# A diffusion layer on one core: modulation steps bound to the matmul units, fewer beside the up-projection and more beside the channel projections

## The chip, the cores and the metric

One Trainium2 chip, one of its cores. The metric is the device time of one execution in microseconds (us); less is better. TensorE (PE) does the matmuls, VectorE (DVE) and ScalarE (ACT) the arithmetic around them, GpSimd (POOL) some of it, SyncE (SP) issues the transfers.

## The reference

One layer over 1024 tokens of width 1024, with 256 context tokens beside them: a half-step SwiGLU feed-forward (ffn1, inner width 2816), a mix of a Fourier group and a two-directional state-space scan (SSD), and a second half-step SwiGLU (ffn2). Each of the three is wrapped in RMS norms and in a modulation that comes from the conditioning vector:

```
mod = (silu(c) @ ada_w + ada_b)           # 9 vectors of 1024
h   = rms_norm(x, g_pre) * (1 + scale) + shift
y   = (silu(h @ w_gate) * (h @ w_up)) @ w_down
x   = x + 0.5 * gate * rms_norm(y, g_post)
```

Everything is computed to float32 accuracy.

## The kernel before

**Products.** A float32 product is made of three matmuls on rounded halves (`mm3`, L461). So every operand is split first: `split` casts the high half on ACT (L198) and subtracts it on DVE for the low half (L199). The up-projection works in 22 *units* of 84 matmuls of 128x512 by a Strassen-like scheme (the products in PSUM `pa` to `pd`); weights come in by `uload`, their sums are made in `usums` (L534 to L537), their splits in `usplit`. `u_first` (L569) is the first DVE addition that takes a unit's products out of PSUM, `u_mid` and `u_late` the rest.

**Start** (L339 to L422). Four iterations i load and transpose token blocks, scale them (L357 on ACT, L359 on DVE), form sums of blocks on DVE (`h_sums`, L396 to L399) and split them (`h_split`): two casts on ACT, 1536 and 2048 wide (L416), and two subtractions (L422), the first on GpSimd, the second on DVE. Then the first products follow (`product(0, p, (i,))`).

**Modulation.** The vectors 0 and 1 are made in the start. The other seven are cut into 14 *u* of 512 columns, made by the generator `ada()`, on DVE. Each u has 8 steps k: a step loads a 128x512 piece of `adaR` (256 KB) into `ring` and multiplies and adds it into an accumulator (L766 for k = 0, else L768), for both streams v if u < 6 and for one after that. When a u is complete, `cut` splits the accumulator (ACT L713, DVE L714), and `end` sums it over the partitions with two matmuls into `pmod` (L720, L721) and writes the vector's place: for mods 2, 5 and 8 with two DMAs (L725, L730), else by DVE into the columns `AB`. Each call of `next(st)` goes one step on. In `ffn_up`, `step()` is called five times per unit; this covers u 0 to 11, until nothing is left. In `ffn_down` one `next(st8)` follows each inner block, for u 12 and 13.

**Down-projection.** `ffn_down` runs three passes over the tokens, tiles (0, 1), (2, 3, 4) and (5, 6, 7), each over the 22 inner blocks f. `down_prep` loads a weight block (512 KB) and a piece of g and splits both, as far ahead as `wring` and `gring` have areas, but never past the end of the pass. After a tile's last block, `post_norm` (L790, L791) reads its PSUM and `pre_scale`, `pre_turn` (L813 transposes, L820) prepare the tile for the mix.

**Channel projections.** `project` runs 24 groups of 24 matmuls (`pch`, 128x256): four token ranges j times six weights i. Each group is copied out by ACT (L986, L988).

**Order.** The program is written in one sequence. A tile scheduler that simulates it fixes each engine's own order of instructions at build time; `high_priority` and `issue_after` bend that order. Every engine then runs its list in order and waits at semaphores.

Of the kernel before, what the change touches and what calls it, by code (L numbers as in the profile page):

```python
# [127 lines left out]
class Kernel:  # L128
# [272 lines left out]
    def h_split(self, i, hb, highs, lows, first):  # L401
# [8 lines left out]
        for o, e in ((0, 3), (3, 7)):  # L410
# [199 lines left out]
    def ffn_up(self, begun, tail, step=lambda: None):  # L610

        n = len(self.ulist)
        for u in range(n):
# [28 lines left out]
            step()  # L642
# [27 lines left out]
    def ffn_down(self, post, step=lambda p, f: None, before=lambda p: None):  # L670

        m = self.m
        P = {}
# [23 lines left out]
    def ada(self, us, ring, acc, sp, scr, ahead, tag="AUX"):  # L697
# [19 lines left out]
        def end(u, v, s):  # L717
            mod, half = 2 + u // 2, u % 2
            P = self.psum("pmod", tag)
# [34 lines left out]
        for n in range(ahead):  # L754
            load(n)
        for n, (u, k) in enumerate(todo):
# [72 lines left out]
    def ffn1(self):  # L829
# [10 lines left out]
        st = self.ada(range(12), ring, acc, sp, scr, 2)  # L840
        st8 = None
# [15 lines left out]
        self.ffn_up(True, tail, lambda: next(st, None))  # L857
# [3 lines left out]
        m.free(self.cc, *self.hfree, *self.wq["S4"])  # L861
# [8 lines left out]
        ring, acc, sp = Ring(m, 512, 2, F32, X2), Ring(m, 512, 1, F32, F0), Ring(m, 1024, 1, FR, X1)  # L870
        st8 = self.ada((12, 13), ring, acc, sp, scr, 1)
        self.pending = []

        def before(p):
            if p == 0:
                state["G"] = self.gload(0)
            if p < 2:
                return

            for _ in st8:  # L880
                pass
            sp.release()
            for r in (self.wring, self.gring):
                for q in r.areas:
                    for s in q:
                        if s[0] is X1:
                            m.free(s)
                r.areas = [q for q in r.areas if q[0][0] is not X1]
            self.gring.areas += [(m.alloc(384, FR, X1), m.alloc(384, FR, Q))]
            state["w"] = [tuple(m.alloc(1024, FR, R0 if i < 2 else X1) for _ in range(2)) for i in range(6)]  # L890
# [3 lines left out]
        def step(p, f):  # L894
            next(st8, None)
# [17 lines left out]

        self.ffn_down(post, step, before)
        for r in (ring, acc, b2, self.graw, self.wraw):
            r.release()
        m.free(state["G"], scr)
# [917 lines left out]
```

## Time and profile before

| | |
|---|---|
| Time, median of 3 runs | 2336.15 us (2334.01 to 2337.88) |
| The profiled execution, its own time | 2346.82 us |
| Its span in the trace | 2344.8 us |
| Mean granted TensorE clock | 0.966 |
| PE / DVE / ACT / POOL busy, share of the span | 92% / 64% / 39% / 18% |

How to read it: busy is the time in which an engine executes. Matmuls are pipelined, so a busy PE can still run below its pace; the count of matmuls per us in a stretch shows that. The granted clock is a share of 2.4 GHz; at 0.5 the engine runs at 1.2 GHz. The rest of the execution's time, 2346.82 - 2344.8 = 2.0 us, lies around the span.

### The profile page before, as it was taken

The numbers are of one execution on the slowest core, as the hardware profiler recorded it, in microseconds if no ns is written. First come the engines' busy times: TensorE is split into PE (matmuls) and PEld (weight loads), VectorE is DVE, ScalarE is ACT, GpSimd is POOL, SyncE is SP. The second block draws the span as 40 slices with busy tenths as digits, with TensorE's granted clock in tenths as the row PEclk, the third lists the DMA queues.
The fourth block names the chain that finished last, engine by engine and source line by source line (L and its number), as shares of the span: only waits on it lengthen the run. The fifth ranks groups of instructions, "written<-read, shape, count | busy, mean of one in ns | idle before, by whom it ended". The sixth has DMA issues, their size and how long they took to land. (4 is left out here: it accounts for less than half of the span.)

```text
span 2344.8 us, 28370 instructions
## 1 busy us (share of the span) xinstructions
PE 2168.8 (92%) x10532; PEld 1805.8 (77%) x10532; DVE 1505.1 (64%) x2226; ACT 924.3 (39%) x1403; POOL 422.6 (18%) x444
## 2 busy tenths in 40 slices
PE   5799999999999899998899987888799999999998
PEld 3577778887778799887888877666688888878886
DVE  6999886656645513348887866787556565656453
ACT  4322223234535433326556545356222222245341
POOL 1100000000212000007776631673000000001010
PEclk9799999999999999999999989999899999999999
DMA  6344553228755501312455445453412222258572
GB/s 259 112 136 153 169 175 99 96 84 276 251 181 192 174 28 47 105 46 90 139 165 178 145 135 166 136 182 122 153 57 85 77 87 75 88 185 275 180 228 88
DMA packets 124827, 329.39 MB, mean 140 GB/s; under 512 B 12928, under 2 KB 43776, under 8 KB 123664
## 3 DMA queue, kind: packets, MB, share of 16 engines
q1 hardware_dynamic: 124688, 327.57, 42.8%
q8 instruction: 83, 1.36, 0.2%
q14 instruction: 56, 0.46, 0.1%
HBM read 273.77 MB, written 53.76 MB: 140 GB/s over the span
## 5 line engine op out<-in xcount | busy, mean ns | idle before, releaser
L198 ACT CAST R<-F 128x1024 fp32r<-128x1024 f32 (+1 forms) x172 | 164.3, 961 | 242.5 <-PE pd L461 75.1
L199 DVE TENSOR_TENSOR R<-F,R 128x1024 fp32r<-128x1024 f32 (+1 forms) x155 | 196.3, 1271 | 79.4 <-ACT R L198 72.7
L207 POOL TENSOR_SCALAR F<-F 128x1 f32<-128x1 f32 x18 | 4.2, 235 | 1279.7 <-ACT F L228 1279.7
L198 ACT CAST Q1a<-F 128x1024 fp32r<-128x1024 f32 (+1 forms) x115 | 129.3, 1130 | 225.8 <-PE pd L461 102.7
L461 PE MATMUL pch<-R 128*128 128x512 f32 (+1 forms) x912 | 172.2, 349 | 13.8 <-DVE X3b L790 4.7
L461 PEld LDWEIGHTS pch<-R 128*128 128x128 f32 x912 | 148.1, 198 | 33.9 <-issue 10.3
L461 PE MATMUL gu<-R 128*128 128x256 f32 (+1 forms) x1152 | 162.2, 299 | 2.7 <-ACT R L198 1.2
L461 PEld LDWEIGHTS gu<-R 128*128 128x128 f32 x1152 | 149.8, 194 | 11.2 <-ACT R L198 1.6
L199 DVE TENSOR_TENSOR Q1a<-F,Q1a 128x1024 fp32r<-128x1024 f32 x93 | 113.5, 1220 | 39.0 <-ACT Q1a L198 38.8
L1253 POOL TENSOR_TENSOR R<-F 128x384 fp32r<-128x384 f32 x128 | 128.6, 1033 | 24.2 <-PE pD L1287 17.5
L461 PE MATMUL y<-Q1a 128*128 128x512 f32 x438 | 107.7, 395 | 0.0
L461 PE MATMUL pa<-R,Q1a 128*128 128x512 f32 x330 | 95.6, 401 | 10.9 <-ACT Q1a L198 9.6
L461 PE MATMUL pa<-R 128*128 128x512 f32 x306 | 87.5, 403 | 14.1 <-ACT R L198 13.3
L461 PE MATMUL y<-Q1a,X3a 128*128 128x512 f32 x360 | 93.2, 404 | 5.5 <-DVE X3b L790 2.6
L768 DVE SCALAR_TENSOR_TENSOR X3b<-X3b,F 128x512 f32<-128x512 f32 x126 | 95.1, 770 | 4.2 <-DMA X3b<-adaR 3.9
L461 PEld LDWEIGHTS y<-Q1a 128*128 128x128 f32 x438 | 83.3, 191 | 18.2
L198 ACT CAST X7a<-F 128x1024 fp32r<-128x1024 f32 (+1 forms) x47 | 57.8, 1231 | 90.9 <-PE pd L461 78.5
L461 PE MATMUL pc<-R,Q1a 128*128 128x512 f32 x286 | 87.6, 401 | 0.7 <-DVE F L604 0.7
L461 PEld LDWEIGHTS y<-Q1a,X3a 128*128 128x128 f32 x360 | 68.9, 193 | 22.9 <-issue 3.0
L461 PE MATMUL pd<-R,Q1a 128*128 128x512 f32 x286 | 84.9, 393 | 0.0
L461 PEld LDWEIGHTS pa<-R,Q1a 128*128 128x128 f32 x330 | 62.1, 191 | 29.1 <-ACT Q1a L198 12.1
L199 DVE TENSOR_TENSOR X7a<-F,X7a 128x1024 fp32r<-128x1024 f32 (+1 forms) x47 | 68.1, 1451 | 24.7 <-ACT X7a L198 24.6
(424 smaller groups left out, 4911.1 us busy)
## 6 DMA issues: line engine op xcount, KB each, us to landing
F<-ffn_wd SPq DMA_DIRECT2D x154, 512.0 KB, 4.3
F<-ffn_w SPq DMA_DIRECT2D x42, 1024.0 KB, 5.4
X3b<-adaR SPq DMA_DIRECT2D x112, 256.0 KB, 2.9
F<-ffn_w SPq DMA_DIRECT2D x44, 512.0 KB, 4.4
F<-w_ch SPq DMA_DIRECT2D x26, 512.0 KB, 4.1
g_d<-X3b SPq DMA_DIRECT2D x22, 512.0 KB, 2.7
g_d<-F SPq DMA_DIRECT2D x20, 512.0 KB
X3b<-g_d SPq DMA_DIRECT2D x44, 192.0 KB, 5.8
```

What stands on the lines that cost most here:

```text
L198: nc.scalar.copy(out=m.r(hi, off, off + n), in_=m.f(src, soff, soff + n))
L199: (E or nc.vector).tensor_tensor(out=m.r(lo, off, off + n), in0=m.f(src, soff, soff + n), in1=m.f(hi, off, off + n), op=ALU.subtract)
L207: V.tensor_scalar(out=mv, in0=ss, scalar1=scale * RSQ_M, scalar2=EPS * RSQ_M, op0=ALU.mult, op1=ALU.add)
L461: self.nc.tensor.matmul(out=outs[c], lhsT=l, rhs=r[c], start=first and ps == 0, stop=last and ps == 2, skip_group_check=again)
L768: V.scalar_tensor_tensor(out=ac, in0=m.f(x), scalar=s, in1=ac, op0=ALU.mult, op1=ALU.add)
L1253: G.tensor_tensor(out=m.r(R, 384 * i, 384 * i + 384).rearrange("p (h l) -> p h l", h=3), in0=self.cst(tri).unsqueeze(1).broadcast_to([128, ...
```

## The change

1. `h_split` makes all low halves on DVE (five instructions come from GpSimd: four iterations, of which the third has two).
2. Beside `ffn_up` only u 0 to 7 are made. Each step is issued under `issue_after(self.mark)`, the mark being the unit's `u_first` addition, and one of the five calls per unit goes.
3. u 8 to 13 are made in `project`, three steps after each group of `pch`; their `pmod` takes PSUM from AUX, then from TR. The loads use three buffers, two ahead.
4. `down_prep` may run on into the next pass. `before(p)` is asked when the preparation reaches pass p.
5. The areas of `wring` and `gring` are kept in a list that rotates, and new ones are put at its front. ffn2's down-projection uses the same code.

```diff
@@ h_split
-                    (nc.gpsimd if o == 0 else nc.vector).tensor_tensor(
+                    nc.vector.tensor_tensor(
@@ u_first
-        self.nc.vector.tensor_tensor(out=U, in0=self.P[u, "B"], in1=U, op=ALU.add)
+        self.mark = self.nc.vector.tensor_tensor(out=U, in0=self.P[u, "B"], in1=U, op=ALU.add).ins
@@ ffn_up
             self.u_mid(u)
-            step()
@@ ffn_down
-            before(p)
...
-                while self.nq < min((p + 1) * NF, p * NF + fs[0] + min(len(self.wring.areas), len(self.gring.areas))):
+                while self.nq < min(len(self.passes) * NF, p * NF + fs[0] + min(len(self.wring.areas), len(self.gring.areas))):
+                    if self.nq % NF == 0 and self.nq not in asked:
+                        asked.add(self.nq)
+                        before(self.nq // NF)
+                        continue
                     self.down_prep()
@@ ada
-            P = self.psum("pmod", tag)
+            P = self.psum("pmod", self.adatag)
...
         for n in range(ahead):
             load(n)
+        yield
@@ ffn1
-        st = self.ada(range(12), ring, acc, sp, scr, 2)
+        self.adatag = "AUX"
+        st = self.ada(range(8), ring, acc, sp, scr, 2)
+        next(st)
+
+        def beside():
+            with self.tc.issue_after(self.mark):
+                next(st, None)
...
-        self.ffn_up(True, tail, lambda: next(st, None))
+        self.ffn_up(True, tail, beside)
...
-        ring, acc, sp = Ring(m, 512, 2, F32, X2), Ring(m, 512, 1, F32, F0), Ring(m, 1024, 1, FR, X1)
-        st8 = self.ada((12, 13), ring, acc, sp, scr, 1)
...
         def before(p):
-            if p == 0:
-                state["G"] = self.gload(0)
...
-            for _ in st8:
-                pass
-            sp.release()
...
+            if p == 2:
+                for r in (self.wring, self.gring):
+                    state.setdefault("x1", []).extend(x for q in r.areas if q[0][0] is X1 for x in q)
+                    r.areas = [q for q in r.areas if q[0][0] is not X1]
         def step(p, f):
-            next(st8, None)
+            if p == 2 and f == 0:
+                m.free(*state["x1"])
+                self.gring.areas.insert(0, (m.alloc(384, FR, X1, True), m.alloc(384, FR, Q)))
+                state["w"] = [tuple(m.alloc(1024, FR, R0 if i < 2 else X1) for _ in range(2)) for i in range(6)]
...
+        state["G"] = self.gload(0)
         self.ffn_down(post, step, before)
@@ pairs
-        self.wring.areas += [tuple(m.alloc(1024, FR, bank) for _ in range(2)) for _ in range(nw)]
+        self.wring.areas[:0] = [tuple(m.alloc(1024, FR, bank) for _ in range(2)) for _ in range(nw)]
@@ project
+        scr, ring, acc, sp = m.alloc(1024, F32, self.F0), Ring(m, 512, 2, F32, self.X2), Ring(m, 512, 1, F32, self.F0), Ring(m, 1024, 1, FR, self.Q)
+        ring.areas.append(m.alloc(512, F32, self.F0))
+        st = self.ada(range(8, 14), ring, acc, sp, scr, 2)
+        next(st)
...
                 if j < 2 and i in (1, 4) and self.pending:
                     self.pending.pop(0)()
+                for _ in range(3):
+                    next(st, None)
...
         self.banks(main=1, PZ=4, TR=2)
+        self.adatag = "TR"
+        for _ in st:
+            pass
@@ class Pairs
-        self.areas, self.i = [], 0
-    next = Ring.next
+        self.areas = []
+    def next(self):
+        self.areas.append(self.areas.pop(0))
+        return self.areas[-1]
```

Three places show how the order moves. First, DVE in the start's fourth iteration, from the split of the third iteration's last part to that of the fourth (`X3b` are modulation pieces and accumulators, `X3a` the fourth iteration's halves). Before:

```order
L766 TENSOR_SCALAR X3b<-X3b,F_61 128x512 x2
L359 TENSOR_SCALAR F_61<-ptr,F_61 128x512
L768 SCALAR_TENSOR_TENSOR X3b<-X3b,F_61 128x512 x2
L396 TENSOR_TENSOR F_61<-F_61 128x512
L768 SCALAR_TENSOR_TENSOR X3b<-X3b,F_61 128x512 x2
L397 TENSOR_TENSOR F_61<-F_61 128x512
L768 SCALAR_TENSOR_TENSOR X3b<-X3b,F_61 128x512 x2
L398 SCALAR_TENSOR_TENSOR F_61<-F_61 128x512
L768 SCALAR_TENSOR_TENSOR X3b<-X3b,F_61 128x512 x2
L399 TENSOR_TENSOR F_61<-F_61 128x512
L768 SCALAR_TENSOR_TENSOR X3b<-X3b,F_61 128x512 x4
L422 TENSOR_TENSOR X3a<-F_61,X3a 128x2048
```

Now:

```order
L422 TENSOR_TENSOR Q1a<-F_61,R_60 128x2048
L359 TENSOR_SCALAR F_61<-ptr,F_61 128x512
L396 TENSOR_TENSOR F_61<-F_61 128x512
L397 TENSOR_TENSOR F_61<-F_61 128x512
L422 TENSOR_TENSOR X3a<-F_61,X3a 128x1536
L398 SCALAR_TENSOR_TENSOR F_61<-F_61 128x512
L399 TENSOR_TENSOR F_61<-F_61 128x512
L422 TENSOR_TENSOR X3a<-F_61,X3a 128x2048
L569 TENSOR_TENSOR F_61<-pb,F_61 128x512
```

The modulation's accumulations, two to four between each of the sums, are gone from here, and the first split (1536 wide) has come in from GpSimd between L397 and L398.

Second, DVE where pass 1 of ffn1's down-projection ends and pass 2 begins (128x1024 to L199 is a weight block, 128x384 a piece of g; L790 and L791 read the finished tiles; L793 and L794 now). Before:

```order
L199 TENSOR_TENSOR X3a<-F_61,X3a 128x1024
L199 TENSOR_TENSOR Q1a<-F_61,Q1a 128x1024 x2
L790 SCALAR_TENSOR_TENSOR X3b<-y,F_61 128x1024
L199 TENSOR_TENSOR R_60<-F_61,R_60 128x1024
L791 TENSOR_TENSOR X3b<-X3b,F_61 128x1024
L199 TENSOR_TENSOR Q1a<-X3b,Q1a 128x384
L199 TENSOR_TENSOR Q1a<-F_61,Q1a 128x1024
L199 TENSOR_TENSOR Q1a<-X3b,Q1a 128x384
L790 SCALAR_TENSOR_TENSOR X3b<-y,F_61 128x1024
L199 TENSOR_TENSOR Q1a<-X3b,X3a 128x384
L791 TENSOR_TENSOR X3b<-X3b,F_61 128x1024
L790 SCALAR_TENSOR_TENSOR X3b<-y,F_61 128x1024
```

Now:

```order
L199 TENSOR_TENSOR Q1a<-X3b,Q1a 128x384
L199 TENSOR_TENSOR Q1a<-F_61,Q1a 128x1024 x2
L199 TENSOR_TENSOR Q1a<-X3b,X3a 128x384
L199 TENSOR_TENSOR Q1a<-F_61,Q1a 128x1024
L793 SCALAR_TENSOR_TENSOR X3b<-y,F_61,X3b 128x1024
L794 TENSOR_TENSOR X3b<-X3b,F_61 128x1024
L199 TENSOR_TENSOR R_60<-F_61,R_60 128x1024
L199 TENSOR_TENSOR Q1a<-X3b,Q1a 128x384
L793 SCALAR_TENSOR_TENSOR X3b<-y,F_61,X3b 128x1024
L794 TENSOR_TENSOR X3b<-X3b,F_61 128x1024
L793 SCALAR_TENSOR_TENSOR X3b<-y,F_61,X3b 128x1024
L794 TENSOR_TENSOR X3b<-X3b,F_61 128x1024
```

Four splits for the next pass now stand ahead of the first tile's addition and three tiles' additions stand closer together; before, the splits for pass 2 stood between and behind these.

Third, PE in the channel projections (`pch`; `ptr` are the transposes of the last tiles; `pmod` the sums of a u). Before:

```order
L461 MATMUL pch<-R_60 128x256 x48
L813 MATMUL ptr<-F_61 128x128 x8
L461 MATMUL pch<-R_60,X3a 128x256 x48
L813 MATMUL ptr<-F_61 128x128 x2
L461 MATMUL pch<-R_60,X3a 128x256 x24
L813 MATMUL ptr<-F_61 128x128 x2
L461 MATMUL pch<-R_60,X3a 128x256 x2
L813 MATMUL ptr<-F_61 128x128 x4
L461 MATMUL pch<-R_60,X3a 128x256 x22
```

Now:

```order
L461 MATMUL pch<-R_60 128x256 x48
L816 MATMUL ptr<-F_61 128x128 x8
L461 MATMUL pch<-R_60,X3a 128x256 x53
L722 MATMUL pmod<-Q1a,R_60 128x512
L461 MATMUL pch<-R_60,X3a 128x256
L723 MATMUL pmod<-Q1a,R_60 128x512
L461 MATMUL pch<-R_60,X3a 128x256 x33
L816 MATMUL ptr<-F_61 128x128 x4
L461 MATMUL pch<-R_60,X3a 128x256 x9
L461 MATMUL pch<-R_60 128x256 x6
L816 MATMUL ptr<-F_61 128x128 x4
L461 MATMUL pch<-R_60 128x256 x39
```

The first two matmuls of `pmod`, for u 8, stand after the 101st and 102nd `pch` matmul; those for the other five u follow at some 85 `pch` matmuls from one to the next (after 189, 274, 360, 439 and 516 of the 576). PE executes its list in order, so `pch` behind a `pmod` waits with it.

## Rows read from the trace of the kernel before

**Rows 1.** The page: span, and busy time of each engine.

```profile
span 2344.8 us, 28370 instructions
PE 2168.8 (92%) x10532; PEld 1805.8 (77%) x10532; DVE 1505.1 (64%) x2226; ACT 924.3 (39%) x1403; POOL 422.6 (18%) x444
```

**Rows 2.** Busy time by stretch: from:to, length, busy us (instructions), clock, DMA, GB/s.

```profile
core 0: us, PE busy (x) PEld busy (x) DVE busy (x) ACT busy (x) POOL busy (x), PEclk, DMA share, GB/s
0.00:92.00 92.00, 48.64 (x272) 31.86 (x273) 70.90 (x115) 35.83 (x41) 14.76 (x9) 0.82 0.54 196
92.00:330.00 238.00, 225.90 (x951) 180.50 (x950) 222.43 (x324) 68.61 (x83) 0.00 (x0) 0.98 0.48 159
330.00:535.00 205.00, 205.00 (x894) 167.67 (x893) 129.65 (x162) 61.70 (x73) 0.00 (x0) 1.00 0.30 99
535.00:618.00 83.00, 79.67 (x336) 63.82 (x335) 55.76 (x74) 38.08 (x56) 10.56 (x28) 0.98 0.88 298
690.00:712.00 22.00, 16.84 (x61) 12.67 (x60) 11.51 (x12) 10.16 (x17) 13.25 (x32) 0.84 0.62 217
799.00:830.00 31.00, 23.28 (x162) 23.07 (x163) 16.09 (x41) 16.52 (x29) 5.40 (x9) 0.83 0.45 141
830.00:885.00 55.00, 55.00 (x457) 54.99 (x457) 8.35 (x14) 14.62 (x32) 0.00 (x0) 1.00 0.10 30
```

**Rows 3.** Timeline of POOL in the start: start us, us, instruction, idle before and releaser.

```profile
32.53 3.50 POOL L422 TENSOR_TENSOR R<-F,R 128x1536 fp32r<-128x1536 f32 x1 [32.09 <-ACT R L416]
75.54 3.58 POOL L422 TENSOR_TENSOR X3a<-F,X3a 128x1536 fp32r<-128x1536 f32 x1 [11.79 <-ACT X3a L416]
```

**Rows 4.** Timeline of DVE in the start.

```profile
30.98 1.75 DVE L199 TENSOR_TENSOR R<-F,Q1a 128x1536 fp32r<-128x1536 f32 x1
32.98 3.60 DVE L396 TENSOR_TENSOR F<-F 128x512 f32<-128x512 f32 x1
36.62 0.69 DVE L397 TENSOR_TENSOR F<-F 128x512 f32<-128x512 f32 x1
...
66.97 2.28 DVE L422 TENSOR_TENSOR Q1a<-F,R 128x2048 fp32r<-128x2048 f32 x1
...
75.75 4.58 DVE L768 SCALAR_TENSOR_TENSOR X3b<-X3b,F 128x512 f32<-128x512 f32 x2
...
87.35 2.28 DVE L422 TENSOR_TENSOR X3a<-F,X3a 128x2048 fp32r<-128x2048 f32 x1
```

**Rows 5.** Timeline of ACT in the start's fourth iteration.

```profile
69.35 1.45 ACT L357 ACTIVATE F<-ptr,F 128x512 f32<-128x512 f32 x2 [3.13 <-DVE Q1a L422]
73.99 1.47 ACT L416 CAST X3a<-F 128x1536 fp32r<-128x1536 f32 x1 [3.19 <-issue]
84.81 1.90 ACT L416 CAST X3a<-F 128x2048 fp32r<-128x2048 f32 x1 [9.35 <-DVE F L399]
```

**Rows 6.** Timeline of PE at the end of the start.

```profile
86.76 0.80 PE L461 MATMUL pb<-X3a,Q1a 128*128 128x512 f32 x1 [6.37 <-ACT X3a L416]
```

**Rows 7.** DVE time of the accumulations (L768) in a stretch of the up-projection.

```profile
110.00:150.00 40.00, 13.69 (x20) 1.00 0.45 152
```

**Rows 8.** Waits of PE, 95 to 535 us: engine, line, releaser, total, times, longest.

```profile
PE pa L461 <- ACT Q1a L198: 9.6, 6, 2.8
```

**Rows 9.** Waits of PE, 535 to 600 us.

```profile
PE pmod L720 <- ACT X3a L713: 3.3, 2, 2.6
```

**Rows 10.** Timeline of DVE in pass 0: first and last of one u's eight accumulations.

```profile
547.15 0.49 DVE L766 TENSOR_SCALAR F<-X3b,F 128x512 f32<-128x512 f32 x1 [2.03 <-DMA X3b<-adaR]
...
566.38 0.75 DVE L768 SCALAR_TENSOR_TENSOR F<-X3b,F 128x512 f32<-128x512 f32 x1
```

**Rows 11.** Waits of PE, 798 to 890 us.

```profile
PE pch L461 <- DVE X3b L790: 4.7, 1, 4.7
PE pch L461 <- ACT F L988: 3.6, 1, 3.6
```

**Rows 12.** The page's DMA issues: transfers, KB each, us from issue to landing.

```profile
X3b<-adaR SPq DMA_DIRECT2D x112, 256.0 KB, 2.9
```

More of the change, by code (lines that the diff above doesn't have):

```diff
@@ L672, in ffn_down @@
         m = self.m
-        P = {}
+        P, asked = {}, set()
         def mm(q, p, i, t):
@@ L694, in ffn_down, with ada @@
                     step(p, f)
-    def ada(self, us, ring, acc, sp, scr, ahead, tag="AUX"):
+    def ada(self, us, ring, acc, sp, scr, ahead):
         m, nc, a = self.m, self.nc, self.a
@@ L855, in tail @@
             self.down_prep()
-        self.ffn_up(True, tail, lambda: next(st, None))
+        self.ffn_up(True, tail, beside)
         for r in (self.ut, self.sg):
             r.release()
-        m.free(self.cc, *self.hfree, *self.wq["S4"])
+        m.free(self.cc, scr, *self.hfree, *self.wq["S4"])
         self.hh = [m.alloc(4096, FR, R0) for _ in range(2)]
@@ L869, in ffn1 @@
         b2 = Ring(m, 1024, 2, F32, X2)
-        ring, acc, sp = Ring(m, 512, 2, F32, X2), Ring(m, 512, 1, F32, F0), Ring(m, 1024, 1, FR, X1)
-        st8 = self.ada((12, 13), ring, acc, sp, scr, 1)
         self.pending = []
         def before(p):
-            if p == 0:
-                state["G"] = self.gload(0)
-            if p < 2:
-                return
-            for _ in st8:
-                pass
-            sp.release()
[L883 to L890, printed above, removed]
+            if p == 2:
+                for r in (self.wring, self.gring):
+                    state.setdefault("x1", []).extend(x for q in r.areas if q[0][0] is X1 for x in q)
+                    r.areas = [q for q in r.areas if q[0][0] is not X1]
         self.wch = []
         def step(p, f):
-            next(st8, None)
+            if p == 2 and f == 0:
+                m.free(*state["x1"])
+                self.gring.areas.insert(0, (m.alloc(384, FR, X1, True), m.alloc(384, FR, Q)))
+                state["w"] = [tuple(m.alloc(1024, FR, R0 if i < 2 else X1) for _ in range(2)) for i in range(6)]
             i = len(self.wch)
@@ L912, in post @@
             self.pending.append(lambda: self.pre_turn(2, m.r(self.hh[c]), m.r(self.hl[c]), 512, (t % 4) * 128, xx, self.full, "AUX", True, V if t > 5 else None))
+        state["G"] = self.gload(0)
         self.ffn_down(post, step, before)
-        for r in (ring, acc, b2, self.graw, self.wraw):
+        for r in (b2, self.graw, self.wraw):
             r.release()
-        m.free(state["G"], scr)
+        m.free(state["G"])
         for r in (self.wring, self.gring):
@@ L924, in pairs @@
         m = self.m
-        self.wring.areas += [tuple(m.alloc(1024, FR, bank) for _ in range(2)) for _ in range(nw)]
-        self.gring.areas += [tuple(m.alloc(384, FR, bank) for _ in range(2)) for _ in range(ng)]
+        self.wring.areas[:0] = [tuple(m.alloc(1024, FR, bank) for _ in range(2)) for _ in range(nw)]
+        self.gring.areas[:0] = [tuple(m.alloc(384, FR, bank) for _ in range(2)) for _ in range(ng)]
     def tok_proj(self, P, n, t, ws):
@@ L1001, in project @@
         self.banks(main=1, PZ=4, TR=2)
+        self.adatag = "TR"
+        for _ in st:
+            pass
+        for r in (ring, acc, sp):
+            r.release()
+        m.free(scr)
         for w in self.wch:
```

1 line of the change is left out of this document (removed).

## The prediction

> **What bounds the kernel now.** I read the page first, then the time by stretch, and last the waits and timelines of the stretches in which something is lost. TensorE is busy in 92% of the span, VectorE in 64% [rows 1], so the end is set by TensorE nearly everywhere, and the change can win only where TensorE runs below its pace. The pace is seen from 330 to 535 us, where the up-projection goes on after the modulation's steps have run out: 894 matmuls in 205 us, 4.36 per us, without a gap and at the full clock [rows 2]. A unit of 84 matmuls then takes 84 / 4.36 = 19.3 us. Held against that pace, the other stretches lose:
>
> - 0 to 92 us: PE is busy 48.6 us, DVE 70.9; the stretch is bound by loads and by the chain over DVE and ACT.
> - 92 to 330 us: 951 matmuls are worth 951 / 4.36 = 218 us; 238 went by, so 20 are lost. VectorE is busy in 222 of the 238 us, with the accumulations among it: 20 in 40 us [rows 7].
> - 535 to 618 us: 336 are worth 77 us, 83 went by: 6 lost, at a DMA share of 0.88.
> - 690 to 712 us: 61 are worth 14 us: 8 lost, and the clock falls to 0.84.
> - 799 to 830 us: 7.7 us of 31 without a matmul, and a clock of 0.83; the same kind of work runs at 457 matmuls in 55 us from 830 on, so 162 are worth 19.5 us: 11.5 lost [all rows 2].
>
> From 885 us on the change touches little: only the down-projection of ffn2 runs through the edited code.
>
> The profiled execution took 2346.8 us, 10.7 more than the median of the three runs, 2336.15. The terms come from the profiled one; I take the sum off both.
>
> **The start: -13 us (bounds -5 and -18).** In the fourth iteration the last split of the third ends at 66.97 + 2.28 = 69.25 us and the fourth's own last split at 87.35 + 2.28 = 89.63 [rows 4]: 20.4 us. Two things fill it. The accumulations stand between the sums in VectorE's list, and one pair of them took 4.58 us [rows 4], where ten accumulations take 6.8 [rows 7], because GpSimd was subtracting from 75.54 to 79.12 [rows 3]. Both go. What is left is a chain: two activations 1.45 and a cast 1.47 [rows 5], to 72.2; the split of 1536 columns, now on VectorE, 1.75 (the same width and form in L199) [rows 4], to 73.9; two sums of 0.69, to 75.3; the cast of 2048, 1.90 [rows 5], to 77.2; the split of 2.28, to 79.5. With half a us for handing over that is 80, 9.6 less than 89.6. TensorE waited for just this cast and split [rows 6], so all of it counts. In the first three iterations one sum each took some 3.6 us in place of 0.69, beside a GpSimd subtraction of 3.5 [rows 3, 4]: 2.9 saved three times, and a split of 1.75 added to VectorE three times, which makes about -3.4. Together -13. The weakest end is the fourth iteration's half, -5, if loads come next in line; the strongest is -18, if the later products no longer meet the low clock of 0.82.
>
> Here a rule speaks against the change. The Trainium skill ("Perfetto Trace Analysis", section "Optimizing Scalar/DVE Operations") says that when VectorE is saturated, moving some work off to ScalarE or even GpSimd may make sense, and adds that GpSimd shares a port with it; the trace agrees with the second half (3.60 against 0.69 us [rows 4]) and I go by that.
>
> **Beside the up-projection: -12 us (bounds -4 and -20).** Removed are the accumulations of u 8 to 11, 32 x 0.68 = 22 us of VectorE, and their cuts; the other 64 are spread: two per step for both streams, at most four steps and so 8 accumulations per unit. Without accumulations VectorE needs, from 92 to 330 us, 222.4 - 238 / 40 x 13.7 = 141 us for 951 / 84 = 11.3 units, 12.5 us per unit; eight accumulations add 5.5, so 18.0 of 19.3 us. Before it was 12.5 + 7.2 = 19.7 us per unit, more than the pace allows, and the unit took 21. PE's longest waits here are for splits whose VectorE half is late too, 9.6 us by the release of ACT [rows 8]. All 20 us come back if VectorE at 93% is never late at the wrong moment. I take 12, since a list run in order at that share still makes some splits late, and since the binding to `u_first` keeps accumulations behind the work that TensorE waits for. The lower end, -4, is the case in which less than half of those recorded waits go. On SP 32 loads of `adaR` leave this stretch; the two small DMAs for each half of mods 2 and 5 stay, and of those of mod 8 the four go to SP's queue behind the channel projections, where only ffn2's end reads what they write.
>
> **Into pass 0: -5 us (bounds 0 and -7).** The first `pmod` waits, 3.3 us, go from here [rows 9], and so does the traffic of the sixteen `adaR` pieces, 4 MB, at a share of 0.88. Six us are lost in this stretch; I take 5.
>
> **From pass 1 to pass 2: -7 us (bounds 0 and -8).** The splits of pass 2's first blocks now stand ahead of the reads of the finished tiles on VectorE, with their loads issued earlier on SP; 8 us are lost there now [rows 2]. One us stays for the second block, whose area comes free only with pass 1's last matmuls. What is late next is the PSUM of the tiles: the three of pass 1 fill it, so pass 2's first tile cannot begin before L793 has read pass 1's first, and L793 now has a split of 1.2 us (the 1024-wide form, by width from 1.75 for 1536) more ahead of it. If that read was the bound all along, nothing is won: the end at 0.
>
> **Channel projections: +8 us (bounds -4 and +30).** 48 accumulations at 0.75 us [rows 10], 36 us, and some 15 us for cuts and ends come to VectorE, which has 24 us of work in the 86 us from 799 to 885 [rows 2]. That fits by the sum. But the order fixes PE's `pmod` at some 85 `pch` matmuls from one u to the next, 85 x 55 / 457 = 10.2 us: eight steps must run in 1.3 us each. A step's load takes 2.9 us from issue to landing [rows 12], and with three buffers three steps come in 2.9 us and one accumulation, 1.2 us per step: just enough. Every step late pushes all `pch` behind the `pmod`. Against that, the first copy `pch` waits for, 3.6 us [rows 11], may come earlier. The last tiles' additions and their splits share VectorE with the first accumulations, and the third token range needs those tiles. I take +8: a delay of about one u's length less what the copy gains. The upper end is half of rival D.
>
> The rest is taken as 0 +- 5: ffn2's down-projection through the new order of areas, and scheduler's shifts in the scan.
>
> Sum: -13 - 12 - 5 - 7 + 8 = -29. From the median, 2336.15 - 29 = **2307 us**; the profiled execution would take 2318.
>
> **The rivals.**
>
> - *B, the channel projections hide it all*: the loads are ahead, `pmod` never waits. The +8 becomes 0: 2299 us. For it: DVE is idle in 47 of the 55 us from 830 on [rows 2]. Against: the step has no slack by the estimate above.
> - *C, VectorE still bounds the up-projection*: 18.0 of 19.3 us is close. If its list runs late all the same, the term is 0 to -2 in place of -12: 2318 us.
> - *D, slower*: the modulation in the channel projections goes at the rate that it shows in pass 0. There eight accumulations ran from 547.15 to 567.13 us, 2.7 us each with their loads [rows 10]. Then 48 x (2.7 - 1.3) = 67 us are added behind the fixed `pmod`: 2336 - 37 + 67 = 2366 us. It decides from the step time at which the gain of 37 is used up, 37 / 48 + 1.3 = 2.1 us. For it: the transfers queue on SP behind the stores of the last tiles. Against: pass 0 had two buffers and a DMA share of 0.88, the channel projections three and 0.10 to 0.45 [rows 2].
> - *E, VectorE is the start's bound*: the five splits add 1.75 x 3 + 1.9 = 7 us to its list and nothing is won: 2336 - 29 + 13 + 7 = 2327 us. This is the case of the page named above. Against: of the fourth iteration's 20 us VectorE alone needs 5 for sums and splits once the accumulations are out.
>
> **How the numbers follow.** Forecast 0.60, B 0.16, C 0.10, D 0.08, E 0.06. The range runs from 2294 (B with the start at its better bound) to 2328 (C and E held, D left out). About 0.2%, 4.7 us, is what a measurement of this kernel can tell from no change. Slower by more than that is D, 0.08; the same takes mixtures of C, E and a smaller D, 0.07; faster is the rest, 0.85.
>
> **What would show it.** Right: in the start no VectorE sum above 1 us and the first `u_first` some 10 us earlier; up-projection stretches at over 4.25 matmuls per us with the accumulations in eights; no `pmod` in pass 0; no gap over 2 us between passes 1 and 2; `pmod` waits in the channel projections of some 8 us in all, released by the cut of the accumulator on ACT or VectorE. Wrong: `pmod` waits there of over 30 us (D); splits of the up-projection as late as before (C); a first unit that begins where it began (E).

## The result and the profile after

The changed kernel takes 2310.38 us (median of 4 runs, 2308.27 to 2313.36), the kernel before 2337.02 (4 runs). The ratio is 0.9879, with an interval of 0.9847 to 0.9912: 28 us faster, give or take 8. The forecast was 2307, in a range of 2294 to 2328. The profiled execution of the changed kernel took 2308.27 us with a span of 2306.3.

The page's first part, after:

```profile
span 2306.3 us, 28361 instructions
PE 2151.5 (93%) x10532; PEld 1795.3 (78%) x10532; DVE 1500.8 (65%) x2231; ACT 922.3 (40%) x1403; POOL 410.9 (18%) x439
```

The engines' sums hardly move against [rows 1]; PE has the same 10532 matmuls in a span that is 38.5 us shorter. What is shorter shows by stretch (after; the columns as in [rows 2]; the stretches are cut at the same places of the program, so at other times):

```profile
0.00:76.50 76.50, 42.16 (x270) 26.47 (x271) 54.51 (x102) 36.45 (x41) 0.20 (x4) 0.90 0.57 210
76.50:330.00 253.50, 253.50 (x1100) 206.68 (x1099) 220.82 (x309) 75.82 (x92) 0.00 (x0) 1.00 0.40 131
330.00:498.00 168.00, 168.00 (x732) 137.23 (x731) 112.29 (x145) 50.08 (x60) 0.00 (x0) 1.00 0.33 108
498.00:582.00 84.00, 84.00 (x367) 68.11 (x366) 49.59 (x61) 43.26 (x63) 11.66 (x28) 1.00 0.78 257
650.00:676.00 26.00, 24.29 (x111) 19.14 (x110) 15.39 (x18) 16.25 (x26) 17.21 (x40) 1.00 0.64 219
...
749.00:790.00 41.00, 30.64 (x213) 29.29 (x213) 30.17 (x65) 18.53 (x33) 6.47 (x9) 0.88 0.72 225
790.00:844.00 54.00, 49.67 (x404) 48.40 (x404) 36.81 (x63) 13.30 (x31) 0.00 (x0) 1.00 0.58 175
```

In the second row PE is busy without a gap, at the full clock, at 1100 / 253.5 = 4.34 matmuls per us: the up-projection has reached the pace that it had before only after the modulation's end. The last two rows are the channel projections, where PE now has gaps and VectorE is busy more than before.

For all kernels the same six places were read from the timelines: the start of the first L569, of the first `y`, of the first `pch`, of the first `pz`, of ffn2's first `pa`, and of the last matmul. The stages between them, in us, each from one profiled execution, and the time as a ratio to the kernel before:

| kernel | start | up | down | channels | mix | rest | ratio, interval |
|---|---|---|---|---|---|---|---|
| before | 91.3 | 442.5 | 269.4 | 78.7 | 806.1 | 645.2 | |
| before again (e0) | 94.2 | 440.8 | 271.7 | 76.4 | 806.3 | 641.8 | 1.0007 (0.9995 to 1.0019) |
| after | 76.2 | 422.0 | 254.6 | 90.9 | 809.8 | 641.0 | 0.9879 (0.9847 to 0.9912) |
| e1 splits on GpSimd | 84.5 | 422.1 | 254.5 | 88.0 | 802.5 | 641.1 | 0.9856 (0.9836 to 0.9875) |
| e2 before, splits on DVE | 81.1 | 433.9 | 267.4 | 76.0 | 811.5 | 643.0 | 0.9948 (0.993 to 0.9966) |
| e3 not bound | 81.1 | 430.3 | 255.3 | 90.5 | 796.1 | 640.5 | 0.9888 (0.987 to 0.9907) |
| e4 no preparation across | 74.4 | 422.2 | 254.7 | 89.9 | 811.9 | 642.6 | 0.9873 (0.9855 to 0.9891) |
| e5 u 0 to 11 bound | 74.1 | 436.6 | 256.4 | 82.3 | 809.5 | 641.4 | 0.9884 (0.9868 to 0.99) |
| e6 one load per u | 74.4 | 423.5 | 254.5 | 82.6 | 817.4 | 642.7 | 0.9841 (0.9818 to 0.9864) |
| e8 u 0 to 9, two steps | 74.6 | 424.5 | 254.5 | 83.9 | 806.7 | 641.7 | 0.9835 (0.9818 to 0.9852) |
| e10 early areas | 76.5 | 422.5 | 254.6 | 88.7 | 808.7 | 641.3 | 0.9848 (0.9832 to 0.9864) |
| e11 old list order | 76.4 | 422.1 | 259.5 | 90.1 | 808.4 | 642.3 | 0.9896 (0.9875 to 0.9917) |
| e12 copies at high priority | 74.6 | 423.4 | 254.6 | 84.0 | 804.9 | 641.4 | 0.9827 (0.9806 to 0.9848) |
| e13 behind the last rstd | 76.4 | 423.5 | 254.7 | 82.9 | 809.9 | 641.5 | 0.9844 (0.9826 to 0.9861) |

The stages down and rest repeat within some 4 us where no edit touches them (down: 254.5 to 254.7 in six kernels). How well one program repeats is shown by three pairs that have, in their traces, the same list of instructions on every engine: before and e0, after and e4, e8 and e12. Their stages differ by up to 3.4, 2.1 and 1.8 us. The mix goes from 796 to 817 us, and no edit is in it. There after, e4 and e11 have one order (808.4 to 811.9 us) and e8, e12 and e13 another (804.9 to 809.9); e1, e3 and e6, which lie outside, each have an order of their own. So the order that the scheduler chose goes with the larger differences; that it makes all of them is not shown. A theory is judged by its own stage, and the ratio only beside it.

The changed kernel's stages against before: -15.1, -20.5, -14.8, +12.2, +3.7, -4.2: the 38.7 us between the two profiled executions. Against e0, the second profile of before, they are -18.0, -18.8, -17.1, +14.5, +3.5, -0.8: 36.7 us. The ratio gives 28, since the execution of before that was profiled first, 2346.8 us, was a long one, and that of the changed kernel the shortest of its four.

**Where the gains and the loss lie.** VectorE in the start (after):

```profile
32.60 0.68 DVE L396 TENSOR_TENSOR F<-F 128x512 f32<-128x512 f32 x1
33.20 1.75 DVE L422 TENSOR_TENSOR R<-F,R 128x1536 fp32r<-128x1536 f32 x1
...
67.47 1.76 DVE L422 TENSOR_TENSOR X3a<-F,X3a 128x1536 fp32r<-128x1536 f32 x1
...
72.53 2.29 DVE L422 TENSOR_TENSOR X3a<-F,X3a 128x2048 fp32r<-128x2048 f32 x1 [1.96 <-ACT X3a L416]
```

The sum L396 that took 3.60 us [rows 4] takes 0.68, and the split beside it 1.75 in place of GpSimd's 3.50 [rows 3]. The fourth iteration's last split ends at 74.8 in place of 89.6.

The waits of PE in the channel projections, 748 to 850 us (after):

```profile
PE pch L461 <- ACT F L992: 5.6, 2, 4.5
PE pch L461 <- DVE X3b L793: 3.9, 1, 3.9
PE pmod L722 <- ACT Q1a L715: 3.4, 3, 1.3
PE pch L461 <- ACT X3b L995: 0.9, 1, 0.9
PE ptr L816 <- ACT X3b L821: 0.6, 1, 0.6
PE ptr L816 <- DVE F L735: 0.3, 1, 0.3
```

They make 14.7 us, against 8.3 in [rows 11]. The third row is the chain that was feared, and it is short: three waits, for the last three u. The first row is the larger part and was there before with 3.6.

### The profile page after: what moved, and what is told of

Read it like the earlier page. It is cut to its first block, busy times and chain, and to the rows that moved or that the text cites. A ratio compares the mean times of both kernels' runs of the same rounds, so it can differ in the third digit from the quotient of the medians.

```text
span 2306.3 us, 28361 instructions
## 1 busy us (share of the span) xinstructions
PE 2151.5 (93%) x10532; PEld 1795.3 (78%) x10532; DVE 1500.8 (65%) x2231; ACT 922.3 (40%) x1403; POOL 410.9 (18%) x439
## 4 chain that ended last, share of the span: by engine, by line
PE 72%; DVE 10%; DMA 8%; issue 4%; ACT 3%; POOL 3%; SPq 0%; DVEq 0%; POOLq 0%; ACTq 0%
PE y L461 21%; PE pa L461 10%; PE pc L461 10%; PE pd L461 10%; PE pb L461 5%; PE pch L461 5%; PE pz L461 3%; PE gu L461 3%; DMA X3b<-adaR 1%; DVE R L199 1%; PE pwo L461 1%; DVE F L1311 1%; DMA F<-ffn_w 1%; DMA X2a<-ada 1%; POOL R L1265 1%
## 5 line engine op out<-in xcount | busy, mean ns | idle before, releaser
L199 DVE TENSOR_TENSOR R<-F,R 128x1024 fp32r<-128x1024 f32 (+1 forms) x155 | 194.7, 1260 | 92.5 <-ACT R L198 85.4
L199 DVE TENSOR_TENSOR Q1a<-F,Q1a 128x1024 fp32r<-128x1024 f32 x92 | 112.3, 1221 | 33.7 <-ACT Q1a L198 33.1
L1265 POOL TENSOR_TENSOR R<-F 128x384 fp32r<-128x384 f32 x128 | 126.3, 1015 | 21.7 <-PE pD L1299 15.1
L461 PEld LDWEIGHTS y<-Q1a 128*128 128x128 f32 x432 | 80.5, 188 | 18.8 <-DVE Q1a L199 0.8
L198 ACT CAST X7a<-F 128x1024 fp32r<-128x1024 f32 (+1 forms) x48 | 58.9, 1229 | 90.1 <-PE pd L461 78.4
L461 PE MATMUL y<-Q1a,X3a 128*128 128x512 f32 x348 | 86.8, 396 | 0.0
L461 PE MATMUL y<-X7a 128*128 128x512 f32 x330 | 79.4, 396 | 2.9 <-ACT X7a L198 2.9
L199 DVE TENSOR_TENSOR X7a<-F,X7a 128x1024 fp32r<-128x1024 f32 (+1 forms) x48 | 69.4, 1446 | 18.5 <-ACT X7a L198 17.6
L461 PEld LDWEIGHTS pa<-R 128*128 128x128 f32 x306 | 58.5, 192 | 27.0 <-ACT R L198 12.5
L534 DVE TENSOR_TENSOR F<-F 128x1024 f32<-128x1024 f32 x42 | 51.4, 1225 | 41.8 <-DMA F<-ffn_w 41.5
```

The lines of the kernel that those rows point to most:

```text
L198: nc.scalar.copy(out=m.r(hi, off, off + n), in_=m.f(src, soff, soff + n))
L199: (E or nc.vector).tensor_tensor(out=m.r(lo, off, off + n), in0=m.f(src, soff, soff + n), in1=m.f(hi, off, off + n), op=ALU.subtract)
L461: self.nc.tensor.matmul(out=outs[c], lhsT=l, rhs=r[c], start=first and ps == 0, stop=last and ps == 2, skip_group_check=again)
L534: V.tensor_tensor(out=m.f(e).rearrange("p (s c) -> p s c", s=2), in0=s[1].unsqueeze(1).broadcast_to([128, 2, 512]), in1=m.f(w, 0, 2048).re ...
L1265: G.tensor_tensor(out=m.r(R, 384 * i, 384 * i + 384).rearrange("p (h l) -> p h l", h=3), in0=self.cst(tri).unsqueeze(1).broadcast_to([128, ...
```

## The experiments

All times and stages stand in the table; each run is told with what it was to show.

**e0_before_again**: the kernel before, unedited.

> The kernel before, once more, for a second profiled execution. The first one took 2346.8 us where the median is 2336, and the spans of the two kernels differ by 38.5 us where the medians differ by 27. Theory: the extra 10 us of that execution lie in single stretches (waits for loads in the start, half-clock stretches in the up-projection), and a second profile shows the start's end (first L569) some us earlier than 91.3 us or an up-projection with fewer half-clock stretches; the time is 2334 to 2340. Rival: the trace of before is typical, and the second one agrees with it within 2 us at every stage.

It took 2343.56 us (10 runs), its span 2342.8. The stages agree with the first profile's within 3.4 us each, with signs both ways. So no single stretch of the first profile was an accident: this kernel's executions lie between 2332 and 2349 us in all, and the first profile was taken from the upper part. The time of 2334 to 2340 that the theory expected did not come; the rival, "typical", holds, but to 3 us and not to 2.

**e1_gpsimd_split and e2_vsplit_alone**: the start's two edits apart. e1 takes the split back from the changed kernel, e2 puts it alone into the kernel before:

```diff
-                    nc.vector.tensor_tensor(
+                    (nc.gpsimd if o == 0 else nc.vector).tensor_tensor(
```

> The changed kernel with the first splits of the start back on GpSimd; the accumulations stay out of the start. Theory (the two engines hold each other up, 2.9 us at one VectorE sum per iteration): four such sums of 3 us and more come back in the start, against 7 us of splits that leave VectorE; the first L569 comes 3 to 6 us later than 76.2, and the time is 3 to 6 us more, 2313 to 2316. Rival (VectorE's own work is the start's bound, so the splits cost what they take): the start gets 5 to 7 us shorter, 2304. Second rival (only the accumulations mattered): no difference over 1 us at the first L569.

> The kernel before with one part of the change alone, the first splits of the start on VectorE; the accumulations stay between the fourth iteration's sums. Theory: the three long sums and the long pair of accumulations (4.6 us) go, 1.75 us per split comes: the first L569 comes 3 to 6 us earlier than in before, and the time is 3 to 6 us less. Rival (VectorE bound): 0 to 7 us later. What is left of the 15 us of the start is then the accumulations' part.

In e1 the start is 8.3 us longer than in after (10.1 than in e4, its repeat); the long sums are back. VectorE, e1:

```profile
33.56 3.60 DVE L396 TENSOR_TENSOR F<-F 128x512 f32<-128x512 f32 x1
...
75.06 3.79 DVE L399 TENSOR_TENSOR F<-F 128x512 f32<-128x512 f32 x1
```

GpSimd, e1:

```profile
33.12 3.50 POOL L422 TENSOR_TENSOR R<-F,R 128x1536 fp32r<-128x1536 f32 x1 [32.68 <-ACT R L416]
...
74.43 3.87 POOL L422 TENSOR_TENSOR X3a<-F,X3a 128x1536 fp32r<-128x1536 f32 x1 [8.63 <-ACT X3a L416]
```

Each long sum ends half a us after GpSimd's subtraction (37.16 and 36.62; 78.85 and 78.30 us). In e2 the start is 10.2 us shorter than in before (13.1 than in e0), although the accumulations still stand between the sums. So both edits count: with the accumulations in place, the splits' move is worth 10 to 13 us; without them, 8.3; taking the accumulations out is worth 5 to 10 (91.3 or 94.2 to 84.5 in e1 is 7 to 10; 81.1 to 76.2 is 5). The size that was expected, 3 to 6 us, was too small in both. The time of e1 hides this: 2306.59 us, not the 2313 to 2316 expected; its mix stage is 7.3 us shorter than in after, in another order, which neither theory is about.

In e2 the up-projection is 7 to 9 us shorter too, with waits of 5.8 us for splits in place of some 11; why a move in the start does so much there was not followed up, beyond that its order is another. The changed kernel does not owe its gain there to it: in e1 the up-projection takes 422.1 us with the splits on GpSimd.

**e3_unbound and e5_u12_bound**: the up-projection. e3 takes the binding away and keeps u 0 to 7; e5 keeps the binding and puts u 8 to 11 back:

```diff
 e3
-            with self.tc.issue_after(self.mark):
-                next(st, None)
+            next(st, None)
 e5
-        st = self.ada(range(8), ring, acc, sp, scr, 2)
+        st = self.ada(range(12), ring, acc, sp, scr, 2)
-        st = self.ada(range(8, 14), ring, acc, sp, scr, 2)
+        st = self.ada(range(12, 14), ring, acc, sp, scr, 2)
```

> The changed kernel, u 0 to 7 beside the up-projection as now, but without the binding of each step to its unit's first addition; the scheduler may put them where it likes. Theory (the binding matters: accumulations that run early stand in the way of the start's sums and of the splits): the fourth iteration of the start has accumulations between its sums again, the first L569 comes 3 to 8 us later than 76.2, and 3 to 10 us of PE waits for splits come back between there and 330 us; time 2315 to 2325. Rival (only the number of accumulations matters): the up-projection stays without a wait, time within 4 us of 2310.

> The changed kernel with u 0 to 11 beside the up-projection, bound as now, and only u 12 and 13 in the channel projections. Theory (it is the binding and the rate of 8 per unit that freed the up-projection, not the removal of u 8 to 11): the up-projection stays without a wait until its last unit, where the left-over steps pile up in front of the last products' sums and cost 0 to 8 us; the channel projections go back by 6 to 9 us (four of six pmod pairs gone, with their waits of 3.4 us and 1.8 us of matmuls). Time 2300 to 2312. Rival (the removed work is what freed it): waits come back all along the up-projection, 8 to 16 us in all, time 2312 to 2322.

Waits of PE in e3, 76 to 330 us:

```profile
PE pb L461 <- ACT X3a L416: 4.6, 1, 4.6
PE pa L461 <- ACT Q1a L198: 4.3, 5, 1.8
PE pb L461 <- DVE X3a L422: 1.3, 1, 1.3
PE pa L461 <- DVE Q1a L199: 1.2, 1, 1.2
```

Without the binding the accumulations are back among the start's sums (81.1 us, as in e2) and the waits for splits are back (the second and fourth rows; the others belong to the start); the up-projection takes 8.3 us more, with no more accumulations than in after. They stand closer, though. The accumulations (L771) in stretches of 40 us, in after:

```profile
120.00:160.00 40.00, 10.12 (x14) 1.00 0.35 112
280.00:320.00 40.00, 10.22 (x14) 1.00 0.42 135
```

In e3:

```profile
120.00:160.00 40.00, 17.68 (x25) 1.00 0.50 165
280.00:320.00 40.00, 0.00 (x0) 1.00 0.27 91
```

Counted with L769 from one L569 to the next, after has at most 8 per unit; e3 has up to 17 and is done after ten units, as before had 6 to 17 in twelve. So the binding sets two things, the place behind the unit's first addition and the rate, and e3 undoes both; the runs do not tell them apart. In e5, with half as many steps again at the same eight per unit, the up-projection has no wait at all until its end. So it is the binding that frees it, and the theory holds. The two rows of e5, its waits from 76 to 520 us:

```profile
PE pmod L722 <- ACT X3a L715: 8.6, 1, 8.6
PE y L461 <- ACT X3a L198: 2.2, 1, 2.2
```

There the steps that found no room pile up at the end: one `pmod` waits 8.6 us, and the clock falls (0.73 in that stretch):

```profile
496.00:515.00 19.00, 8.12 (x25) 5.53 (x24) 14.18 (x26) 2.68 (x5) 0.00 (x0) 0.73 0.80 253
```

The up-projection is 14.6 us longer than in after, more than the 0 to 8 expected, and the channel projections 8.6 shorter, as expected. Removing u 8 to 11 is thus needed, but for the end of the up-projection, not for its course. e3's ratio is little worse than after's; in its profile the mix stage is 13.7 us shorter, in another order, but that execution, 2307.38 us, was the shortest of six with a median of 2316.23.

**e4_no_cross_prep, e10_early_areas and e11_list_order**: the down-projection, undone part by part, each on top of the one ahead of it:

```diff
 e4
-                while self.nq < min(len(self.passes) * NF, p * NF + fs[0] + ...
+                while self.nq < min((p + 1) * NF, p * NF + fs[0] + ...
 e10, on e4: the three lines that free and allocate at step(2, 0) moved into before(2)
 e11, on e10
-        self.areas = []
-    def next(self):
-        self.areas.append(self.areas.pop(0))
-        return self.areas[-1]
+        self.areas, self.i = [], 0
+    next = Ring.next
-        self.wring.areas[:0] = [
+        self.wring.areas += [
```

with `gring` likewise.

> The changed kernel with the preparation of down-projection blocks ended at each pass's last block, as before. Theory: the 22 us around the end of pass 1 lose 6 to 8 us again, with PE waits for L198, L199 and L793 there, and the clock falls; the end of ffn2's passes loses the like only if it shows there. Time 6 to 10 us more, 2317 to 2320. Rival (the reading of the finished tiles is the bound): 0 to 2 us more, PE waits there for L793 alone.

> The changed kernel without preparation across passes (as in e4_no_cross_prep), and with the areas of the last pass freed and allocated before the pass's first blocks, as the kernel before does, in place of behind them. In e4 the stretch around the end of pass 1 did not get longer. Theory (what ended its 8 us was that the first two blocks of pass 2 no longer use the area that the last block of pass 1 reads): 5 to 9 us come back there, with waits of PE y for L198, L199 and L793 and a half clock; time 2316 to 2320. Rival (the leaving of u 12 and 13, or the rotation of the list, ended them): 0 to 2 us, time 2309 to 2313.

> The kernel e10_early_areas with the third part of the preparation undone as well: a counter walks the list of areas as before, and new areas are put at its end. Nothing but the leaving of u 12 and 13 then sets ffn1's down-projection apart from the kernel before. Theory (a counter over a list that has just been shortened lands on an area that the last blocks of pass 1 still read; the rotation takes the oldest): first matmul of the down-projection to first pch 260 us or more in place of 254.6, waits of PE y for L198, L199 and L793 of 4 to 6 us between pass 1 and 2 with a half clock; time 6 to 10 us over e10. Rival (the end of pass 1 was late because u 12 and 13 shifted the order of VectorE and of the loads): 254 to 256 us, time within 4 us of e10.

e4 takes 254.7 us, but it undoes nothing: on every engine its list of instructions is that of the changed kernel, so the splits that it was to put back still stand ahead. It shows that permission to prepare past the end of a pass (item 4 of the change) has no part in the order that was built, and it is a repeat of the changed kernel; its theory was not tested. e10 does move instructions and takes 254.6 us: its theory falls. e11 costs 4.9 us. Waits of PE in e11, 640 to 760 us:

```profile
PE pch L461 <- DVE X3b L793: 3.8, 1, 3.8
PE y L461 <- DVE X3b L793: 3.0, 1, 3.0
PE y L461 <- ACT Q1a L198: 1.8, 2, 1.0
PE y L461 <- DVE Q1a L199: 0.3, 1, 0.3
```

The waits of `y` were there in the kernel before (the same stretch):

```profile
PE y L461 <- DVE X3b L790: 2.6, 1, 2.6
PE y L461 <- ACT X3a L198: 1.9, 1, 1.9
PE y L461 <- DVE Q1a L199: 0.6, 1, 0.6
```

In e10 all waits of `y` there make 0.8 us. When VectorE reads pass 1's first finished tile (L793), it has split one weight block and one piece of g less in e11 than in after, e4 and e10 (in before one and two less). The splits of a block in e10 for which e11 has none at that time:

```profile
637.42 0.56 DVE L199 TENSOR_TENSOR Q1a<-X3b,Q1a 128x384 fp32r<-128x384 f32 x1 [1.91 <-ACT Q1a L198]
638.41 1.23 DVE L199 TENSOR_TENSOR Q1a<-F,Q1a 128x1024 fp32r<-128x1024 f32 x1 [0.43 <-ACT Q1a L198]
```

and those with which e11 catches up, behind the reads of two finished tiles:

```profile
657.69 1.21 DVE L199 TENSOR_TENSOR Q1a<-F,Q1a 128x1024 fp32r<-128x1024 f32 x1
658.82 0.55 DVE L199 TENSOR_TENSOR Q1a<-X3b,Q1a 128x384 fp32r<-128x384 f32 x1
```

So in e10 PE has 18 matmuls to do in pass 2 before it waits for the second of these reads:

```profile
653.90 1.10 PE L461 MATMUL y<-Q1a,X3a 128*128 128x512 f32 x4
654.83 3.33 PE L461 MATMUL y<-Q1a 128*128 128x512 f32 x14
658.62 1.17 PE L461 MATMUL y<-Q1a,X3a 128*128 128x512 f32 x4 [0.45 <-DVE X3b L793]
```

In e11 it has two:

```profile
654.15 0.72 PE L461 MATMUL y<-Q1a,X3a 128*128 128x512 f32 x2 [0.71 <-ACT Q1a L198]
657.91 0.75 PE L461 MATMUL y<-Q1a,X3a 128*128 128x512 f32 x2 [3.04 <-DVE X3b L793]
```

The order of the list (item 5), rotation with new areas in front, thus keeps the first blocks of pass 2 from waiting. That the counter lands on areas still being read is argued from the code and was not shown by itself.

The three passes, each from its first `y` to the next one's (pass 2 to the first `pch`), show where the rest lies:

| kernel | pass 0 | pass 1 | pass 2 |
|---|---|---|---|
| before | 67.6 | 97.0 | 104.8 |
| before again (e0) | 71.1 | 95.5 | 105.0 |
| after | 61.3 | 93.6 | 99.7 |
| e11 old list order | 61.3 | 94.4 | 103.8 |

Pass 0 is as short in e11 as in after, and only the leaving of u 12 and 13 is left of the change in e11's down-projection: in pass 0 it is worth 6 to 10 us. The list order is worth 4.1 us in pass 2 and 0.8 in pass 1.

**e6_one_load_per_u**: what sets the pace of the steps in the channel projections.

```diff
+            if us[0] and k:
+                w[n] = w[n - 1]
-            if n < len(todo):
+            if n < len(todo) and not (us[0] and todo[n][1]):
```

> The changed kernel with one adaR load per u in the channel projections in place of eight: all eight steps of a u multiply the piece of k = 0, so 42 of the 48 loads and the pieces k = 1 to 7 are left out there. VectorE's work is the same. Theory (the loads set the pace of the late pmod pairs: 816 to 835 us show VectorE idle for adaR before most accumulations): the three pmod waits of 3.4 us go, and the first copies come earlier since SP no longer has adaR loads ahead of w_zdt; 84 to 87 us for the channel projections in place of 91. Rival (VectorE's list, with the last tiles' work in it, sets the pace): pmod waits stay, 89 to 91 us.

The three `pmod` waits are gone; two waits are left, 3.9 us each, and the stage takes 82.6 us. The loads set the pace. Waits of VectorE for them, 790 to 840 us, in after:

```profile
DVE F L771 <- DMA X3b<-adaR: 7.2, 8, 1.6
...
DVE F L771 <- DMA F<-adaR: 1.7, 4, 0.7
```

Eight steps of a u ran from 813.67 to 823.4 us: 1.2 us each. That is the rate that three buffers and a landing time of 2.8 us were reckoned to give. The other u took 1.2 to 1.6 us per step, and all 48 steps, from 762.5 to 834.2 us, 1.5 on average; PE's order allows 1.3 by count, and the first accumulation came 10 us into the stage.

**e8_u10_two_steps, e12_copies_first and e13_after_rstd**: versions that were meant to beat both kernels.

```diff
 e8
-        st = self.ada(range(8), ring, acc, sp, scr, 2)
+        st = self.ada(range(10), ring, acc, sp, scr, 2)
-        st = self.ada(range(8, 14), ring, acc, sp, scr, 2)
+        st = self.ada(range(10, 14), ring, acc, sp, scr, 2)
-                for _ in range(3):
+                for _ in range(2):
 e12, on e8
+                    with self.tc.high_priority():
                         S.copy(out=m.f(s, 0, n), in_=P[:, 0:n])
 e13, on e8
+                with self.tc.issue_after(rs):
                     for _ in range(2):
                         next(st, None)
+                    with self.tc.issue_after(mark):
                         zload("w_zdt", 408, len(sets["w_zdt"]), self.Q)
```

In e13 `rs` is the last L214 on VectorE ahead of the channel projections and `mark` the second copy of `pch`.

> The changed kernel with u 0 to 9 beside the up-projection and u 10 to 13 in the channel projections, two steps per group of pch in place of three. Theory (VectorE is at 67% in the up-projection's last 168 us, so two more u cost nothing there, and a third less work with more time per step ends the pmod waits in the channel projections): the up-projection takes 422 us as now, the channel projections 84 to 87 in place of 91; time 2303 to 2307. Rival (the channels' extra time is the delay of the first weights and copies behind the adaR loads, which stays): 89 to 91 us there, time 2308 to 2311.

> The kernel e8_u10_two_steps with the copies of pch out of PSUM (L992, L995) at high priority. Theory (the first of them stand on ACT behind a cast that waits for w_zdt, and PE waits 3.5 us for them): that wait and the half clock behind it go, the channel projections take 78 to 81 us in place of 84, time 2295 to 2299. Rival (the pmod order then takes what the copies give): 83 to 85 us, time as e8.

> The kernel e8_u10_two_steps with the accumulations of the channel projections bound behind the last VectorE step of the last tile's scale (L214), and the first w_zdt behind the second copy of pch. In the changed kernel the first accumulation stands in VectorE's list between two such steps and waits 1.8 us for its adaR load; ACT's scaling of the tile (L806) waits for the step, the first copy of pch stands behind it on ACT, and PE waits 3.5 us (e8) to 4.5 us (after) for the copy. Theory (that chain sets the wait): the copy comes some 2 us earlier, the wait falls to under 2.8 us, the channel projections take 80 to 82.5 us in place of 83.9, time 2297 to 2301. Rival (the copy waits for something else, or the later accumulations delay the pmod pairs): 84 us or more, pmod waits over 2 us, time as e8 or above.

e8 takes 2301.26 us, ratio 0.9835: the channel projections 7.0 us less than after, the up-projection 2.5 more. Its waits of PE from 748 to 850 us:

```profile
PE pch L461 <- DVE X3b L793: 3.9, 1, 3.9
PE pch L461 <- ACT F L992: 3.5, 1, 3.5
PE pmod L722 <- ACT X3b L821: 1.6, 1, 1.6
```

The modulation costs one `pmod` wait there now, ended by the copy of a transpose (L821) and no longer by the cut of an accumulator. From 330 to 499 us VectorE carries the two more u at 74% busy, with PE at its pace:

```profile
330.00:499.00 169.00, 169.00 (x737) 137.96 (x736) 124.47 (x166) 51.15 (x62) 0.00 (x0) 1.00 0.40 131
```

e12 shows nothing of its theory: its instructions stand in the same order as in e8 on every engine, the cast of w_zdt in front of the first copy among them. It is a repeat of e8, with 2301.42 us; PE waits 4.4 us for the first copy in it. e13 does move the order: the last scale steps run through on VectorE and the wait for the first copy falls from 3.5 to 2.3 us, but a second one, 1.5 us, appears for another copy, and the stage gains 1.0 us, less than the 1.4 to 3.9 expected and no more than after and its repeat e4 differ by there. Its time, 2304.18, is no better than e8's. e8 stays the version to use: e8 and its repeat have ratios of 0.9835 and 0.9827, after and its repeat 0.9879 and 0.9873. The two stages that e8 touches account for 4.5 us of that, about half; the rest is not assigned.

## Why the prediction was right, and where it was wrong

**The start, -13.** Measured -15.1 by the profiles, inside the bounds. Against e0 it is -18.0, at the bound. The chain was sized by the right rows: last split at 80 forecast for the fourth iteration after an unchanged third; it came at 74.8, because the three earlier iterations gave 4.1 us in place of 3.4 (the third's last split ends at 65.2 us against 69.25) and the fourth needs 9.6 us in place of 10.8. The rule of the Trainium skill that was held against the change ("Perfetto Trace Analysis", section "Optimizing Scalar/DVE Operations") says that moving work from a saturated VectorE to GpSimd may make sense, with a warning that the two share a port. e1, which moves it there, has a start 8.3 us longer, so the trace bears out the warning. Rival E falls by e1 and e2.

**Beside the up-projection, -12.** Right in its mechanism, too small in its size: -20.5, just beyond the bound (-18.8 against e0). The step that failed is the one that let VectorE at 93% still be late for some splits. With the binding it was never late, at 220.82 us of 253.5, 87% busy. The reckoned load was too high as well: 18.0 us per unit of 19.3, measured 220.82 / (1100 / 84) = 16.9. Of the reasons given, the removed work and the spread of the rest to eight per unit behind `u_first`, the runs bear out the second: in e5 u 8 to 11 are back, and there is no wait until the end, while in e3 they are gone, the rest is not spread, and 8 us are lost. (The 64 that are spread are steps; they hold 112 accumulations.) Rival C falls.

**Into pass 0 and from pass 1 to 2, -5 and -7.** Together -14.8 measured against -12. Pass 0 took 6.3 us less (9.8 against e0). The gain at the boundary is some 7 us, 1.9 of wait ahead of pass 2's first `y` and 5.1 in pass 2, and its mechanism is the one forecast: the splits of pass 2's first blocks stand ahead of the reads of the finished tiles, and in e11, where VectorE is one block further back when it reads them, 4.9 us are lost again. The prediction read this from the order and did not say which edit makes it. It is the order of the list (item 5) and not the preparation across passes (item 4), which e4 takes away without a change in the order. Against e0 the two are -17.1, beyond their bounds of -15 together.

**Channel projections, +8.** +12.2 measured, inside the bounds. Of it 6.4 us are waits of PE: 3.4 for `pmod`, which was the mechanism forecast, at some 8, and the rest around the first copies, which were forecast to come earlier and came later. 12 matmuls of `pmod` at 0.23 us (one by the pace), 2.8 us, had moved in from other stages and were not counted; some 3 us are not assigned. Rival D was priced by the right quantity, the time of a step: 1.5 us measured on average, under its 2.7 and under the break-even of 2.1. Rival B falls with the 12 us.

**The rest, 0 +- 5.** The mix took 3.7 us more and the end 4.2 less (0.8 against e0). In the mix one wait of the changed kernel is new (880 to 1650 us, after):

```profile
PE gu L461 <- DVE X5a L512: 6.2, 1, 6.2
```

e1, with the same work there in another order, has 0.6 us of it, and its mix is 7.3 us shorter; e4 and e11, with the order of after, have the 6.2 us again. So this wait belongs to the order, which no term forecast.

The sum of the measured terms is -38.7 between the profiles; the runs say -28. The forecast of -29 was met by the median partly because the up-projection gave 8 us more than forecast while the profile of before was 10 us above its median. For the profiled execution itself 2318 was forecast, and it took 2308.27. The mechanism stands; the closeness of 2307 to 2310 is in part luck, and better than the terms were.

## What to carry to other kernels

Side work on an engine that feeds TensorE is cheap if it is tied to the unit that it stands beside, at a rate that leaves that engine some slack; the same amount of work without the tie, and so without the even rate, cost 8 us here. Splitting it over several stages by their slack (10 u beside the up-projection, 4 beside the channel projections) beat both twelve early (e5, a pile-up with 11 us of waits at the end) and six late (after). Before an edit's worth is read from a time, the order of instructions has to be compared: two edits here, e4 and e12, changed nothing in it. Judge such an edit by the stage that it touches: an untouched stage differed by up to 21 us between builds in which the scheduler had ordered it differently, more than most of the effects.

## What was not expected of the hardware

A GpSimd subtraction of 3.5 us held one VectorE sum of 0.69 us until half a us after its own end, in every iteration of the start (3.60, 3.51, 2.88 and 3.79 us in e1, and 1.64 beside the third iteration's second subtraction). A VectorE copy out of PSUM in the same time took its usual 0.42 us (L342, at 33.23 us in e1). The price in the end was more than the balance on VectorE: 12 us of such stalls in e1, less 7 us of splits that VectorE takes over in the changed kernel, make 5; the start differs by 8.3, and the other 3 are not assigned.
